# One core's hybrid decoder step: a list schedule that fixes the order on all five engines, and low parts of weights made by an accumulating DMA

## The chip, the cores and the metric

The kernel runs on one core of one Trainium2 chip. The metric is device microseconds of one execution. The kernel before takes 1466.67 us (median of 3 runs, 1466.05 to 1466.89). TensorE is called PE here, VectorE DVE, ScalarE ACT, GpSimd Pool and SyncE SP; every engine works through its own queue in order, and waits on semaphores for the others.

## The reference

A step of a decoder of two layers, on a prompt of 1024 tokens and on 8 sampled sequences of 4 new tokens each: 1056 tokens in all. The model is 1024 wide, the inside of a layer 2048.

```python
def lru_layer(x, conv_buf, h0, g, w_in, ...):          # layer 0 (Hawk)
    hn = rmsnorm(x, g)
    u = hn @ w_in                                      # 1024 -> 4096
    xb, z = u[..., :D_INNER], u[..., D_INNER:]
    xb, new_buf = causal_dwconv(xb, conv_buf, conv_w, conv_b)   # 4 taps
    y, h_last = rg_lru(xb, h0, w_a, b_a, w_i, b_i, lam)         # gates per block of 128, then a scan
    return x + (y * silu(z)) @ w_out, new_buf, h_last

def ccm_layer(x, conv_buf, g, w_in, b_in, ...):        # layer 1 (Conformer)
    u = rmsnorm(x, g) @ w_in + b_in                    # 1024 -> 6144
    v, gl, z = u[..., :D_INNER], u[..., D_INNER:2 * D_INNER], u[..., 2 * D_INNER:]
    c, new_buf = causal_dwconv(v * sigmoid(gl), conv_buf, dw_w, dw_b)   # 31 taps
    c = silu(layernorm(c, ln_g, ln_b))
    return x + (c * silu(z)) @ w_out + b_out, new_buf
```

A last RMSNorm follows. Everything is fp32.

## The kernel before, in words

**Tiling.** Channels lie on partitions, tokens on the free axis, in three chunks of 352. A weight matrix is cut into slabs of 128x1024 fp32 (512 KB): 48 for layer 0 (16 for the x branch, 16 for the gate z, 16 for the output) and 64 for layer 1 (16 each for v, its gate g and z, 16 for the output). Slabs are numbered in the order of their use, 0 to 47, 48 to 95, 96 to 111; `seq` holds them.

**Precision.** fp32 products are made of three matmuls in the fp32r type: weights and activations are each split into a high part h (the value rounded to fp32r by a copy) and a low part l (value minus high part), and `mm` (L241 on) adds h·h, h·l and l·h in PSUM. Nearly every matmul is 128x128 by 352 columns.

**Weights.** `w_load` (L211) starts a slab's load on SP into `wraw`. `w_conv` (L221) makes the high part `wh` with an ACT copy and the low part `wl` with a subtraction, on Pool but for three slabs of the start, which are on DVE. 38 slabs of layer 1 are "early": while layer 0 runs, `pre_load` (L328) loads each into `pre`, `pre_low` (L332) makes `preh` on ACT, subtracts it (19 on Pool, 19 on DVE, L336) and stores the low part to DRAM, `wld`; when such a slab is used, `w_load` fetches its low part too, and ACT copies it into `wl`.

**Layer 0.** 16 blocks of 128 channels. A block has an x branch (`xp`: 24 matmuls for each chunk, evacuated by `xb_evac`, L507, then the 4-tap convolution on DVE and ACT, L518 to L535, then `split`, L539, into `xcsh` and `xcsl`), a z branch (`zp`, evacuated with a Silu by ACT, L569), two gates (`gp`, per chunk, each of one 128x128 weight), sigmoids (L582), and a chain of DVE, ACT and Pool operations to the scan (`chain`, L586 to L620), whose result times silu(z) is split into `gsh` and `gsl`. Two blocks at a time go into the output (`op`, named by pair, group and chunk: `op2_4_0` is pair 2, output rows 4, chunk 0), which `out_evac` (L644) adds on DVE to the residual x.

**Layer 1.** Per block: g, v and z products (`yp` for the output), the 31-tap convolution (`tap`, L851; ACT, DVE and Pool share the products and sums), LayerNorm over all 2048 channels, then silu, gate and output in four groups, last the final norm (`y_unit`, L1122, `y_evac`, L1133).

**What sets the order.** The program is written as events, `at(t, fn)`, with times given by hand tables. `flush` (L168) calls them in the order of t. The start (t below 46) and the end are under `manual_schedule`, where engines keep the order of the calls; between them the framework's own scheduler orders each engine's instructions by its estimates.

Of the kernel before, what the change touches and what calls it, by code (L numbers as in the profile page):

```python
# [1333 lines left out]
```

## Time and profile before

| | |
|---|---|
| median of 3 runs | 1466.67 us (1466.05 to 1466.89) |
| span of the profiled execution | 1462.3 us |
| PE busy | 1398.0 us, 96% of the span, 8525 instructions |
| DVE busy | 1161.8 us, 79% |
| ACT, Pool busy | 872.4 and 872.5 us, 60% each |
| DMA over the span | 174.69 MB, mean 119 GB/s |

The profile is of one execution on the chip, 4.4 us less in its span than the median of the runs. "Busy" leaves out register, semaphore and DMA-issuing instructions. A row of windows gives, for a stretch of the span, its length and then busy time and instruction count of PE, of its weight loads (PEld), of DVE, ACT and Pool, then the clock granted to PE (1.00 is full), the busy share of the 16 DMA engines, and GB/s. A row of waits names the instruction that waited, by tile and line, what it waited for, and the total, count and longest in us. A row of one tile or line gives count, then shortest, middle and longest duration in ns and when it ran. A row of DMA issues ends in the middle time from issue to landing in us.

Layer 0 lies between about 34 and 640 us, layer 1's products, convolution and LayerNorm between 640 and 1260, and its output and the end behind that.

### The profile page before, as it was taken

To read this page: it belongs to the slowest core of one execution; us is meant where nothing else is said; L and a number is where in the kernel's file an instruction comes from. 1 tells how busy PE (TensorE), PEld (TensorE's weight loads), DVE (VectorE), ACT (ScalarE), POOL (GpSimd) and SP (SyncE) were. 2 spreads that over 40 slices of the span, in tenths; PEclk is the share of its full clock that TensorE was granted. 3 is DMA by queue.
4 is the path that set the end of the run, shared out by engine and by line. 5 is a ranking of instruction groups with operands and counts; after the bars stand their busy time and mean duration, and the time that the engine had idled before them with its cause. 6 is when DMAs were issued, how large, how long until landed. Compare 5 with 4: busy or idle time off the path is not lost.

```text
span 1462.3 us, 21525 instructions
## 1 busy us (share of the span) xinstructions
PE 1398.0 (96%) x8525; PEld 1367.2 (93%) x8525; DVE 1161.8 (79%) x1274; ACT 872.4 (60%) x1132; POOL 872.5 (60%) x479
## 2 busy tenths in 40 slices
PE   6998999999999999989999999999999999998997
PEld 6998989989899999989999989999999999998997
DVE  5777875675666767668989999999999997988525
ACT  5578466556565566757567676667677655533212
POOL 3544364345454545246689899998888996434233
PEclk9999999999999999999999999999999999999999
DMA  7011143343443342205623325333334224745203
GB/s 262 26 40 52 62 148 134 134 162 119 141 147 129 124 156 110 87 24 182 157 72 92 106 77 205 103 133 110 112 117 141 92 88 131 243 172 189 76 0 119
DMA packets 91829, 174.69 MB, mean 119 GB/s; under 512 B 41648, under 2 KB 53936, under 8 KB 91696
## 3 DMA queue, kind: packets, MB, share of 16 engines
q1 hardware_dynamic: 71152, 170.66, 34.0%
q10 hardware_dynamic: 20576, 2.66, 1.1%
q8 instruction: 67, 1.10, 0.3%
q14 instruction: 34, 0.28, 0.1%
HBM read 128.77 MB, written 46.22 MB: 120 GB/s over the span
## 4 chain that ended last, share of the span: by engine, by line
DVE 25%; PE 22%; POOL 5%; issue 3%; ACT 3%; DMA 2%; SPq 0%; POOLq 0%; DVEq 0%; ACTq 0%
DVE cv__9086 L870 2%; DVE cv__10890 L870 2%; DVE cv__9391 L870 2%; DVE cv__8787 L870 2%; POOL part__7852 L832 1%; DMA co<-od 1%; DVE cv__10602 L870 1%; POOL part__8145 L832 1%; DVE co L1089 1%; DVE cv__7518 L870 1%; DVE cpad L816 1%; DVE cv__9687 L870 1%; DVE cv__11218 L870 1%; DVE cv__8491 L870 1%; DVE co L1085 1%
## 5 line engine op out<-in xcount | busy, mean ns | idle before, releaser
L827 ACT ACTIVATE prod<-cpad,lay 128x1024 f32<-128x1024 f32 x119 | 135.7, 1147 | 64.1 <-POOL part__8145 L832 7.7
L530 DVE SCALAR_TENSOR_TENSOR acc<-pad,par,acc 128x1080 f32<-128x1080 f32 x32 | 62.5, 1961 | 39.6 <-ACT acc L523 39.2
L612 POOL COPY st_h<-r 128x1 f32<-128x1 f32 x16 | 17.4, 1090 | 103.6 <-DVE r L611 103.6
L336 POOL TENSOR_TENSOR pre<-pre,preh 128x1024 f32<-128x1024 f32 x19 | 49.5, 2607 | 48.2 <-ACT preh L335 37.4
L542 POOL TENSOR_TENSOR gsl<-zs,gsh 128x1056 fp32r<-128x1056 f32 x15 | 37.1, 2474 | 26.3 <-ACT gsh L541 23.3
L1152 POOL TENSOR_TENSOR sq<-sq 128x512 f32<-128x512 f32 (+2 forms) x20 | 19.0, 953 | 56.4 <-ACT sq L1148 56.2
L1148 ACT ACTIVATE sq<-x 128x512 f32<-128x512 f32 (+2 forms) x23 | 11.4, 501 | 67.5 <-DVE x L1138 63.6
L336 DVE TENSOR_TENSOR pre<-pre,preh 128x1024 f32<-128x1024 f32 x19 | 30.3, 1593 | 26.2 <-ACT preh L335 26.2
L541 ACT ACTIVATE gsh<-zs 128x1056 fp32r<-128x1056 f32 x15 | 16.3, 1084 | 56.2 <-DVE zs L618 56.2
L541 ACT ACTIVATE xcsh<-xc 128x1056 fp32r<-128x1056 f32 x16 | 17.4, 1086 | 53.6 <-DVE xc L535 53.6
L894 POOL TENSOR_TENSOR sum<-sum,co 128x1056 f32<-128x1056 f32 x13 | 35.0, 2689 | 23.9 <-DVE co L870 15.4
L1093 ACT ACTIVATE co<-co,par 128x352 f32<-128x352 f32 (+1 forms) x24 | 22.7, 970 | 41.8 <-DVE co L1089 41.8
L335 ACT ACTIVATE preh<-pre 128x1024 fp32r<-128x1024 f32 x38 | 40.0, 1052 | 12.8 <-DMA pre<-win 12.6
L400 POOL TENSOR_TENSOR hl<-hn,hh 128x352 fp32r<-128x352 f32 x24 | 25.4, 1062 | 36.5 <-ACT hh L397 31.0
L879 POOL TENSOR_TENSOR smp<-spad,lay 128x992 f32<-128x992 f32 x16 | 40.1, 2504 | 4.3 <-DVE spad L815 4.3
L944 POOL TENSOR_TENSOR ssq<-ssq,sq 128x1056 f32<-128x1056 f32 x14 | 40.6, 2897 | 0.0
L594 DVE TENSOR_TENSOR i<-i,xc 128x1056 f32<-128x1056 f32 x16 | 31.4, 1965 | 10.2 <-ACT i L582 9.1
L604 DVE TENSOR_TENSOR q<-q,i 128x1056 f32<-128x1056 f32 x16 | 21.7, 1356 | 21.9 <-ACT q L601 21.9
L611 DVE TENSOR_TENSOR_SCAN r<-a,q 128x1056 f32<-128x1056 f32 x16 | 37.7, 2357 | 0.6
L1105 POOL TENSOR_TENSOR nl<-co,nh 128x1056 fp32r<-128x1056 f32 x6 | 16.6, 2767 | 34.3 <-ACT nh L1101 31.8
L1085 DVE TENSOR_TENSOR co<-co,mub 128x1056 f32<-128x1056 f32 (+1 forms) x20 | 25.3, 1289 | 10.8 <-DMA co<-od 7.9
L393 DVE SCALAR_TENSOR_TENSOR hn<-x,par,pb 128x352 f32<-128x352 f32 x48 | 25.5, 573 | 9.6 <-PE pb L285 5.2
(5161 smaller groups left out, 6637.2 us busy)
## 6 DMA issues: line engine op xcount, KB each, us to landing
pre<-win SPq DMA_DIRECT2D x38, 512.0 KB, 3.7
wld<-pre SPq DMA_DIRECT2D x38, 512.0 KB, 2.8
zd<-z SPq DMA_DIRECT2D x16, 528.0 KB, 3.0
od<-co SPq DMA_DIRECT2D x12, 528.0 KB, 3.0
zr<-zd SPq DMA_DIRECT2D x12, 528.0 KB, 3.7
co<-od SPq DMA_DIRECT2D x12, 528.0 KB, 5.8
x<-xT SPq DMA_DIRECT2D x24, 176.0 KB, 4.6
x1d<-x SPq DMA_DIRECT2D x8, 528.0 KB, 6.1
```

What stands on the lines that cost most here:

```text
L335: act.activation(h, r, AF.Copy)
L336: (dve if early[i] % PRED == PRED - 1 else pool).tensor_sub(r, r, h.bitcast(F))
L530: dve.scalar_tensor_tensor(acc, pad[:, k:k + n], w, acc, op0=OP.mult, op1=OP.add)
L541: act.activation(h, src, AF.Copy)
L542: lo.tensor_sub(l, src, h.bitcast(F))
L611: dve.tensor_tensor_scan(h, B["a", s], B["q", s], 0.0, op0=OP.mult, op1=OP.add)
L827: act.activation(p, B["c", j][:, k:k + NP], AF.Identity, scale=dw(j, k), bias=P("dw_b", j) if k == 0 else 0.0)
L870: dve.scalar_tensor_tensor(o, x, dw(j, k), y, op0=OP.mult, op1=OP.add)
L879: pool.tensor_mul(t_.rearrange("p (b t w) -> p b t w", b=NB, t=NS), win, wb)
L894: pool.tensor_add(B["sum"], B["sum"], B["o", j])
L944: (dve if j in SQD else pool).tensor_add(B["ssq"], B["ssq"], q)
L1085: dve.tensor_sub(d, d, B["mu", 0][:, :C] if c == 0 else B["mub"][:, w])
```

## The change

**A list schedule.** All operations are now recorded first, each with its engine, the tiles that it reads and writes, and an estimated duration. `schedule` gives every operation a due time, backwards from its users, and then lets the engines take operations one at a time: at each step the operation that can start first, or one more urgent that can start within a short wait. What the planner has free (SBUF slots, PSUM banks) is part of it. The order that comes out is fixed for all five engines, in the whole program. Its costs are numbers in the file; it takes into account that some DVE and Pool operations share an access and cannot run at once (`lock`).

**Low parts by DMA.** Of the 74 slabs whose low part was a subtraction, 69 (from slab 5 on: 43 of layer 0, 6 of layer 1's first, 4 last z slabs, 16 of the output) now have it made by two steps: DVE writes minus the high part into `wl` (one multiplication by -1, one source), and Pool issues a DMA that adds `wraw` to it, SBUF to SBUF. For the 38 early slabs ACT writes minus the high part (scale -1 in the copy) into `preh`, and a Pool-issued DMA adds it to `pre`, which is stored to `wld` as before; at use `wld` is loaded straight into `wl`, without `wlow` and without the ACT copy.

**Beside it.** z is evacuated by three plain copies and one Silu over 1056 tokens (`z_silu`); each gate runs as one piece, 9 matmuls over the three chunks; 90 tiny "spare" activations load ACT tables ahead of their use; the pool `quick` is merged with the slots (44 in all). By instruction counts: DVE loses 19 subtractions and gains 69 multiplications, Pool loses 69 and 19 subtractions and gains 107 accumulating DMAs for weights and 10 for activations, ACT loses 38 copies and gains 16 Silus and the 90 spares, SP loads 38 low parts into another tile. The matmuls are the same ones.

The first place is PE at the gates of block 7, some 303 us into the run before. Names: `zp7_2` is z of block 7, chunk 2; `op2_4_0` is the output of pair 2 (blocks 4 and 5); `wh21`, `wl21` are the parts of slab 21; `gp7` is a gate of block 7 out of the split convolution `xcsh7`. Before:

```order
L246 MATMUL zp7_2__2859<-hh_153,wl20__2663 128x352
L244 MATMUL op2_4_0__2895<-gsh4_2035,wh21__2780 128x352
L245 MATMUL op2_4_0__2895<-gsl4_2036,wh21__2780 128x352
L244 MATMUL op2_4_1__2903<-gsh4_2035,wh21__2780 128x352
L245 MATMUL op2_4_1__2903<-gsl4_2036,wh21__2780 128x352
L244 MATMUL gp7_0__2997<-xcsh7_2848,gwh_2854 128x352
L246 MATMUL op2_4_0__2895<-gsh4_2035,wl21__2782 128x352
L244 MATMUL op2_4_0__2895<-gsh5_2405,wh21__2780 128x352
L245 MATMUL op2_4_0__2895<-gsl5_2406,wh21__2780 128x352
L246 MATMUL op2_4_0__2895<-gsh5_2405,wl21__2782 128x352
```

After, at the gates of the same block:

```order
L379 MATMUL op2_6_1_.0_3011<-gsh4.0_2115,wl21_.0_2794 128x352
L379 MATMUL op2_6_1_.0_3011<-gsh5.0_2530,wh21_.0_2721 128x352
L379 MATMUL op2_6_1_.0_3011<-gsl5.0_2557,wh21_.0_2721 128x352
L379 MATMUL op2_6_1_.0_3011<-gsh5.0_2530,wl21_.0_2794 128x352
L379 MATMUL gp7_0_0_.0_3019<-xcsh7.0_2940,gwh.7_2751 128x352
L379 MATMUL gp7_0_0_.0_3019<-xcsl7.0_2950,gwh.7_2751 128x352
L379 MATMUL gp7_0_0_.0_3019<-xcsh7.0_2940,gwl.7_2754 128x352
L379 MATMUL gp7_0_1_.0_3020<-xcsh7.0_2940,gwh.7_2751 128x352
L379 MATMUL gp7_0_1_.0_3020<-xcsl7.0_2950,gwh.7_2751 128x352
L379 MATMUL gp7_0_1_.0_3020<-xcsh7.0_2940,gwl.7_2754 128x352
L379 MATMUL gp7_0_2_.0_3021<-xcsh7.0_2940,gwh.7_2751 128x352
```

Before, the gate's first matmul stood 4 matmuls after block 7's z and cut into the output of pair 2, whose low-part matmuls followed it. Now it stands 48 matmuls after z, behind whole output products of pair 2, and a gate runs through all its chunks.

The second place is Pool in the same stretch of the program. `pre` rows are low parts of early slabs, `gsl6` the low part of block 6's gated output. Before:

```order
L542 TENSOR_TENSOR gsl6_2770<-zs6_2448,gsh6_2769 128x1056
L336 TENSOR_TENSOR pre_2731<-pre_2731,preh_2773 128x1024
L232 TENSOR_TENSOR wl21__2782<-wraw21__2665,wh21__2780 128x1024
L232 TENSOR_TENSOR wl22__2891<-wraw22__2784,wh22__2889 128x1024
L336 TENSOR_TENSOR pre_2918<-pre_2918,preh_2976 128x1024
L232 TENSOR_TENSOR wl23__3033<-wraw23__2893,wh23__3031 128x1024
```

After; a row with DMA is the issue of an accumulating transfer:

```order
L379 TENSOR_TENSOR gwl.7_2754<-graw.7_2633,gwh.7_2751 128x256
L379 DMA pre.10_2667<-preh.10_2789 128x1024
L379 DMA wl21_.0_2794<-wraw21_.0_2611 128x1024
L379 COPY st_h_75<-r6.0_2676 128x8
L379 COPY st_conv_74<-pad7.0_2635 128x3
L379 COPY st_conv_74<-pad7.0_2635 128x24
L379 COPY st_h_75<-r6.0_2676 128x1
L379 TENSOR_TENSOR gsl6.0_2902<-zs6.0_2526,gsh6.0_2865 128x1056
L379 DMA pre.11_2748<-preh.11_2867 128x1024
L379 DMA wl22_.0_2938<-wraw22_.0_2826 128x1024
```

Five subtractions of 128x1024 stood around `gsl6` before; now only DMA issues, gate weights, small copies of states and the same `gsl6` are left.

The third place is the end of layer 0 after the change, first on Pool, then on PE. `wl46` is the low part of the second output slab of the last pairs (6 and 7), `zp15_2` z of the last block, `op6_4_0` the first output product after it.

```order
L379 DMA wl44_.0_5781<-wraw44_.0_5543 128x1024
L379 DMA wl45_.0_5785<-wraw45_.0_5646 128x1024
L379 TENSOR_TENSOR gsl14.0_5932<-zs14.0_5813,gsh14.0_5928 128x1056
L379 DMA wl46_.0_5938<-wraw46_.0_5747 128x1024
L379 DMA wl47_.0_5971<-wraw47_.0_5750 128x1024
L379 DMA wl48_.0_5991<-wraw48_.0_5926 128x1024
```

```order
L379 MATMUL zp15_2_.0_5940<-hl.7_206,wh44_.0_5672 128x352
L379 MATMUL zp15_2_.0_5940<-hh.7_184,wl44_.0_5781 128x352
L379 MATMUL op6_4_0_.0_6016<-gsh12.0_5118,wh45_.0_5728 128x352
L379 MATMUL op6_4_0_.0_6016<-gsl12.0_5128,wh45_.0_5728 128x352
L379 MATMUL op6_4_0_.0_6016<-gsh12.0_5118,wl45_.0_5785 128x352
L379 MATMUL op6_4_0_.0_6016<-gsh13.0_5504,wh45_.0_5728 128x352
L379 MATMUL op6_4_0_.0_6016<-gsl13.0_5537,wh45_.0_5728 128x352
L379 MATMUL op6_4_0_.0_6016<-gsh13.0_5504,wl45_.0_5785 128x352
L379 MATMUL op6_4_0_.0_6016<-gsh14.0_5928,wh46_.0_5898 128x352
L379 MATMUL op6_4_0_.0_6016<-gsl14.0_5932,wh46_.0_5898 128x352
L379 MATMUL op6_4_0_.0_6016<-gsh14.0_5928,wl46_.0_5938 128x352
```

The number at the end of a tile's name counts tiles as the planner made them: `wl46` (5938) was made just ahead of `zp15_2` (5940), which begins 24 matmuls ahead of `op6_4_0`. The first use of `wl46` is the ninth matmul of `op6_4_0`, so 32 matmuls lie between them. Where the tiles of slabs 5, 9, 12, 47, 49 and 100 were made, between 35 and 50 matmuls lie ahead of the first use; for the others it is mostly more, between about 75 and 140.

The diff, cut to its core:

```diff
-NSLOT = 42  # tiles for whole rows of tokens
-NQUICK = 2
...
+WAHEAD = 1
+NSUB = 5
...
+T_TABLE, T_SEM, T_DMA0, T_DMAX, DMA_BW = 1.3, 0.055, 0.6, 1.25, 290.0e3
...
+    def schedule(self, caps):
...
+            o.due = o.at + SHIFT.get(o.key, 0.0)
+        for o in reversed(ops):
+            for s in o.succ:
+                o.due = min(o.due, s.due - o.dur - MARGIN - (T_DMA0 + T_DMAX + o.dma / DMA_BW if o.dma else 0))
+        queues = {e: sorted((o for o in ops if o.eng == e), key=lambda o: o.due) for e in ENG}
...
+        while todo:
+            best = None
+            lead = queues["PE"][0].due if queues["PE"] else 1e9
+            for e in ENG:
...
+                for i, o in enumerate(queues[e]):
+                    if i >= WIN[e] or (e != "PE" and o.due > lead + LOOK[e]):
+                        break
+                    if o.left:
+                        continue
+                    new = [t for t in o.acc if t.kind and t.place is None]
...
+                    s = max((max(free[e], last_end[e]) + x) if x else free[e], o.ready, c)
+                    if o.lock:
+                        s = max(s, lock)
+                    opts.append((s, x, o))
...
+                pick = opts[0]
+                for q in opts[1:]:
+                    back = T_TABLE if q[1] and pick[2].func and pick[2].func == table else 0.0
+                    if q[0] + q[2].dur + back + q[1] * 0.5 <= pick[0] + FIT[e]:
+                        pick = q
+                        break
+                s, x, o = pick
+                if best is None or s < best[0]:
+                    best = (s, x, o)
...
+            if o.dma:
+                d0 = max(dma, s + o.dur + T_DMA0 - 0.06)
+                dma = d0 + o.dma / DMA_BW
+                o.end = dma + T_DMAX
+            else:
+                o.end = s + o.dur + (0.17 if e == "PE" else 0.09)
+            last_end[e] = max(last_end[e], o.end)
+            if o.lock:
+                lock = s + o.dur - 0.05
...
+ENG = ("PE", "DVE", "Activation", "Pool", "SP")
+WIN = {"PE": 3, "DVE": 30, "Activation": 30, "Pool": 20, "SP": 12}
...
+MARGIN = 0.15
...
-        def flush(t_ordered=1e9):
-            todo = sorted(ev, key=lambda e: e[:2])
-            for engines, a, b in ((SU_E, -1e9, SU_M), ((), SU_M, t_ordered), (MAN, t_ordered, 1e9)):
-                with ExitStack() as order_:
-                    if engines:
-                        order_.enter_context(tc.manual_schedule(
-                            engines={getattr(mybir.EngineType, e) for e in engines}))
-                    for t_, _, fn, args in todo:
-                        if a <= t_ < b:
-                            fn(*args)
-            ev.clear()
...
+        def flush():
+            for i, (t_, _, fn, args) in enumerate(sorted(ev, key=lambda e: e[:2])):
+                plan.at, plan.event = t_, i
+                plan.key = fn.__name__ + (str(args[1]) if fn in (chain, conv0) else "")
+                fn(*args)
+            plan.schedule({"s": NSLOT, "g": NSMALL, "mm": 4, "aux": 4, "c": 1})
+            with tc.manual_schedule(engines={getattr(mybir.EngineType, e) for e in ENG}):
+                plan.emit(make, warm)
...
-                if i in early:
-                    lows[i] = slot(name=f"wlow{i}_", n=1024)
-                    sp.dma_start(lows[i], wld[early[i]])
...
                 if i in early:
-                    act.activation(l, lows.pop(i), AF.Copy)
+                    sp.dma_start(l.bitcast(F), wld[early[i]])
+                elif i < NSUB:
+                    (dve if split else pool).tensor_sub(l, r, h.bitcast(F))
                 else:
-                    (dve if split else pool).tensor_sub(l, r, h.bitcast(F))
+
+                    dve.tensor_scalar(l, h.bitcast(F), -1.0, None, op0=OP.mult)
+                    pool.dma_start(l.bitcast(F), r, accum_op=OP.add)
                 hls[i] = (h, l)
...
-            w_load(n + ahead + 1)
+            w_load(n + ahead + WAHEAD)
...
             r = B.pop(("pre", i))
             h = slot(FR, "preh", 1024)
-            act.activation(h, r, AF.Copy)
-            (dve if early[i] % PRED == PRED - 1 else pool).tensor_sub(r, r, h.bitcast(F))
+            act.activation(h, r, AF.Copy, scale=-1.0)
+            pool.dma_start(r, h.bitcast(F), accum_op=OP.add)
...
-            act.activation(B["zs", s][:, cs(c)], ps[:, :C], AF.Silu)
+            act.activation(B["zs", s][:, cs(c)], ps[:, :C], AF.Copy)
 
         def z_silu(s):
-            act.activation(B["zs", s][:, :C], B["zs", s][:, :C], AF.Silu)
-
-        def gate_unit(s, u):
-            g, c = divmod(u, NCH)
+            act.activation(B["zs", s], B["zs", s], AF.Silu)
+
...
+        def gate_units(s, g):
             h, l = B["gw", s]
             xh, xl = B["xcs", s]
-            ps = aux(f"gp{s}_{u}_")[:, :C]
-            mm(ps, [(h[:, g * 128:g * 128 + 128], l[:, g * 128:g * 128 + 128], xh[:, cs(c)], xl[:, cs(c)])])
-            if c == 0:
-                B["ri"[g], s] = slot(name=f"{'ri'[g]}{s}", n=NT)
-            act.activation(B["ri"[g], s][:, cs(c)], ps, AF.Sigmoid, bias=P("b_a" if g == 0 else "b_i", s))
-            if u == 2 * NCH - 1:
+            B["ri"[g], s] = slot(name=f"{'ri'[g]}{s}", n=NT)
+            ps = [aux(f"gp{s}_{g}_{c}_")[:, :C] for c in range(NCH)]
...
                 act.activation(B["q", s], B["q", s], AF.Sqrt)
+                if s not in late_z:
+                    z_silu(s)
```

More of the change, by code (lines that the diff above doesn't have):

```diff
@@ L1 @@
+import bisect
 import numpy as np
@@ new lines, with __init__, v @@
+class T:
+    def __init__(self, kind, name, shape, dt=F, real=None, phase=0, dram=False):
+        self.kind, self.name, self.dt, self.real, self.phase, self.dram = kind, name, dt, real, phase, dram
+        self.shape, self.left, self.free, self.place = shape, 0, 0.0, None
+        fake = [1 if q == 128 and i == (1 if dram else 0) else q for i, q in enumerate(shape)]
+        self.idx = np.arange(int(np.prod(fake))).reshape(fake)
+        self.users, self.hist = [], []
+    @property
+    def v(self):
+        return V(self, (), self.idx)
@@ new lines, with __init__ @@
+class Op:
+    __slots__ = ("eng", "parts", "due", "t", "pre", "succ", "left", "dur", "lock", "acc", "new", "dma", "start",
+                 "end", "func", "warm", "key", "kind", "n", "at", "ready", "tail")
+    def __init__(self, eng, at):
+        self.eng, self.at, self.parts, self.acc, self.pre, self.succ = eng, at, [], [], set(), []
+        self.dur, self.lock, self.dma, self.new, self.func, self.ready, self.warm = 0.0, False, 0, [], None, 0.0, False
+TABLE = {AF.Sigmoid: 1, AF.Exp: 2, AF.Tanh: 2, AF.Sqrt: 3, AF.Silu: 4}
@@ new lines, with __init__, __getattr__ @@
+class Eng:
+    def __init__(self, plan, name, real):
+        self.plan, self.name, self.real = plan, name, real
+    def __getattr__(self, op):
+        fn = getattr(self.real, op)
+        return lambda *a, **kw: self.plan.record(self.name, op, fn, a, kw)
+ENG = ("PE", "DVE", "Activation", "Pool", "SP")
+WIN = {"PE": 3, "DVE": 30, "Activation": 30, "Pool": 20, "SP": 12}
+LOOK = {"DVE": 20.0, "Activation": 20.0, "Pool": 20.0, "SP": 20.0}
+MARGIN = 0.15
+SHIFT = {}
+FIT = {"PE": 0.1, "DVE": 0.2, "Activation": 0.2, "Pool": 0.4, "SP": 0.1}
@@ L115, in build @@
     nc = tc.nc
-    pe, act, dve, pool, sp = nc.tensor, nc.scalar, nc.vector, nc.gpsimd, nc.sync
+    plan = Plan(tc)
+    pe, act, dve, pool, sp = (Eng(plan, n, e) for n, e in zip(
+        ("PE", "Activation", "DVE", "Pool", "SP"), (nc.tensor, nc.scalar, nc.vector, nc.gpsimd, nc.sync)))
     from contextlib import ExitStack
@@ new lines, in make @@
+        def make(t):
+            if t.kind == "c":
+                return pools["c"].tile(t.shape, t.dt, tag="lay", name=t.name)
+            if t.kind in ("s", "g"):
+                return pools[t.kind].tile([128, SLOT if t.kind == "s" else C], t.dt, tag=f"{t.kind}{t.place}_", name=t.name)
+            if t.kind == "mm":
+                return pools["mm"].tile(t.shape, F, tag=f"mm{t.place}_", name=t.name)
+            if px.get("open") != t.phase:
+                if "ctx" in px:
+                    px.pop("ctx").close()
+                px["ctx"], px["open"] = ExitStack(), t.phase
+                px["pool"] = px["ctx"].enter_context(tc.tile_pool(
+                    name=f"aux{t.phase}_", bufs=1, space=bass.MemoryType.PSUM, reuse_waits="tile"))
+            return px["pool"].tile(t.shape, F, tag=f"a{t.phase}_{t.place}_", name=t.name)
@@ new lines, in build @@
+        par = const("par", [128, PAR], F)
+        ident = const("ident", [128, 128], F)
+        ones = const("ones", [128, 1], F)
+        avg_r = const("avg_r", [128, 128], FR)
+        c8 = const("c8", [128, 2, KI], F)
+        st_conv = const("st_conv", [128, KI, (NB + 1) * (W0 - 1)], F)
+        st_h = const("st_h", [128, KI, NB + 1], F)
+        sm = const("sm", [128, 64], F)
+        x1d = scratch("x1d", [KD, 128, NT])
+        zd = scratch("zd", [KI, 128, NT])
+        od = scratch("od", [KI, 128, NT])
@@ L195, in build @@
+        spare = const("spare", [128, 2])
+        nss = const("nss", [128, NB * NS], F)
+        wld = scratch("wld", [NPRE, 128, D])
         lay = {}
@@ L694, in ev_gate @@
             nonlocal t
-            for u in range(2 * NCH):
-                at(t, gate_unit, s, u)
-                t += 0.45
+            for g in range(2):
+                at(t, gate_units, s, g)
+                t += 1.35
             ds_ = (0.5, 1.6, 4.8, 6.6, 7.2, 8.4, 9.8) if s < KI - 1 else (0.5, 1.6, 4.8, 6.6, 7.2, 10.9, 11.0)
+            if s not in z_end:
+                late_z.add(s)
             f = EARLY if s < 4 else STEADY if s < KI - 1 else 1.0
@@ L732, in build @@
         at(t, softplus)
-        for s in range(2):
-            at(SU_Z + 0.1 * s, z_silu, s)
         wi = 4
```

272 lines of the change are left out of this document (230 added, 42 removed).

## The prediction

> **What bounds the kernel now.** I read the page first: its first line and the busy times.
>
> ```profile
> span 1462.3 us, 21525 instructions
> PE 1398.0 (96%) x8525; PEld 1367.2 (93%) x8525; DVE 1161.8 (79%) x1274; ACT 872.4 (60%) x1132; POOL 872.5 (60%) x479
> ```
>
> PE is busy 96% of the span and the change leaves its matmuls alone, so all that can be won is what PE loses. Where it loses, the windows say (columns: stretch, length, busy time and count of PE, its weight loads, DVE, ACT, Pool; granted clock, DMA share, GB/s).
>
> ```profile
> 0.00:34.20 34.20, 23.26 (x115) 22.36 (x115) 19.02 (x28) 18.40 (x34) 12.01 (x18) 0.90 0.79 280
> 64.00:640.00 576.00, 548.83 (x3345) 540.90 (x3344) 398.26 (x437) 372.02 (x477) 267.28 (x190) 0.99 0.32 113
> 640.00:700.00 60.00, 57.80 (x355) 56.62 (x355) 47.76 (x89) 38.06 (x73) 33.41 (x27) 0.97 0.40 123
> 700.00:800.00 100.00, 100.00 (x625) 99.42 (x624) 93.26 (x80) 62.84 (x74) 79.21 (x33) 1.00 0.40 106
> 700.00:1220.00 520.00, 515.08 (x3158) 504.33 (x3157) 510.51 (x433) 345.02 (x399) 455.45 (x181) 1.00 0.36 113
> 1260.00:1370.00 110.00, 105.05 (x644) 102.64 (x644) 94.88 (x104) 41.73 (x43) 47.35 (x19) 1.00 0.54 193
> ```
>
> In 700 to 800 PE never stops: 100 us for 625 matmuls, 0.160 us each. I price every stretch by that. Layer 0 (64 to 640) needs 3345 x 0.160 = 535.2 of its 576 us: it loses 40.8, of which 576 - 548.83 = 27.2 are idle and 548.83 - 535.2 = 13.6 are matmuls that ran slowly. Layer 1 (700 to 1220) needs 505 of 520, with DVE busy for 510.5: DVE is its bound. 1260 to 1370 needs 103.0 of 110: 7 lost. So the place to argue about is layer 0. PE's waits there name the releasers (total, times, longest):
>
> ```profile
> PE xp__184 L244 <- ACT hh L412: 6.2, 1, 6.2
> PE op__1459 L244 <- DVE x L646: 3.5, 1, 3.5
> PE op__5881 L244 <- ACT gsh L623: 3.4, 1, 3.4
> PE gp__2997 L244 <- ACT xcsh L541: 3.4, 1, 3.4
> ...
> PE op__3671 L244 <- DVE x L646: 2.0, 1, 2.0
> ...
> PE op__5603 L244 <- DVE x L646: 1.9, 1, 1.9
> PE gp__1296 L244 <- ACT r L582: 1.8, 1, 1.8
> ...
> PE op__1861 L244 <- DVE x L646: 1.7, 1, 1.7
> PE op__2551 L244 <- ACT zs L569: 1.5, 1, 1.5
> ...
> PE op__3289 L244 <- ACT zs L569: 1.5, 1, 1.5
> ```
>
> Output products wait until DVE has evacuated a bank, a gate until DVE's convolution has been split. DVE is busy only 69% of layer 0; why is it late? The timeline around the gate of block 7 (start, length):
>
> ```profile
> 292.36 5.90 DVE L530 SCALAR_TENSOR_TENSOR acc<-pad,par,acc 128x1080 f32<-128x1080 f32 x2 [2.39 <-ACT acc L523]
> 293.67 3.44 POOL L336 TENSOR_TENSOR pre<-pre,preh 128x1024 f32<-128x1024 f32 x1
> 297.07 3.42 POOL L232 TENSOR_TENSOR wl__2782<-wraw__2665,wh__2780 128x1024 fp32r<-128x1024 f32 x1
> 298.36 3.22 DVE L533 SCALAR_TENSOR_TENSOR xc<-pad,par,acc 128x1024 f32<-128x1024 f32 x1
> 302.96 0.66 PE L244 MATMUL gp__2997<-xcsh,gwh 128*128 128x352 f32 x1 [3.44 <-ACT xcsh L541]
> ```
>
> and the same lines over the whole run (shortest, middle, longest ns), then the ten microseconds after:
>
> ```profile
> L530 DVE SCALAR_TENSOR_TENSOR acc<-pad,par,acc x32: 1327/1345/3531, 66.6 to 583.7; 128x1080 f32<-128x1080 f32 x32
> L533 DVE SCALAR_TENSOR_TENSOR xc<-pad,par,acc x16: 1271/1285/3339, 72.7 to 585.8; 128x1024 f32<-128x1024 f32 x16
> L336 POOL TENSOR_TENSOR pre<-pre,preh x19: 2388/2411/3485, 185.6 to 579.6; 128x1024 f32<-128x1024 f32 x19
> L336 DVE TENSOR_TENSOR pre<-pre,preh x19: 1206/1226/3423, 186.3 to 596.1; 128x1024 f32<-128x1024 f32 x19
> 300.00:310.00 10.00, 7.04 (x28) 7.04 (x29) 5.51 (x7) 5.99 (x7) 2.92 (x3) 0.66 0.56 210
> ```
>
> Three convolution steps of 1.3 us took 9.1 us because two Pool subtractions ran among them, and those took 3.4 instead of 2.4. The convolution is 5 us late, PE waits 3.4, and then its granted clock is 0.66 for ten microseconds: one wait costs twice.
>
> **The change part by part.** *Subtractions leave Pool (43 + 19 in layer 0) and DVE (19).* At 2.4 to 3.4 us the 62 are 149 to 211 of Pool's 267 us. Waits of the DVE kind (op 1459, gp 2997, op 3671, op 5603, op 1861) sum to 12.5 us. I take four fifths, 10.0: Pool keeps `gsl` and gate work to collide with, but the order after also puts a gate 48 matmuls behind z where it was 4. The ACT kind (gp 1296, op 2551, op 3289) is 4.8 us: the copy of z frees its bank without the Silu table, gates have whole output products ahead; three quarters, 3.6. `gsh` of the last block (3.4) is a chain's end that the change doesn't shorten: 0. The rest of the 27.2, 6.5 in small waits: half, 3.3. That is 16.9 of 27.2, 62%; of the 13.6 of slow matmuls, which follow waits, the same share is 8.4. Layer 0: -25.3 us. Its bounds are 0 and -40.8.
>
> *Negations come to DVE.* The groups of instructions give what goes (busy us, mean ns; then idle time ahead):
>
> ```profile
> L335 ACT ACTIVATE preh<-pre 128x1024 fp32r<-128x1024 f32 x38 | 40.0, 1052 | 12.8 <-DMA pre<-win 12.6 <-POOL wl__2663 L232 0.2
> L336 DVE TENSOR_TENSOR pre<-pre,preh 128x1024 f32<-128x1024 f32 x19 | 30.3, 1593 | 26.2 <-ACT preh L335 26.2
> ```
>
> No row shows a multiplication of one source with 1024 columns. The nearest is the subtraction at 1.2 us. In layer 0 43 x 1.2 = 52 replaces 19 x 1.6 = 30 and the collisions; DVE has 178 us free there, so 0 in itself. In 700 to 1220, where DVE is the bound, the order after has four (slabs 92 to 95): 4 x 1.2 = +4.8. In 1260 to 1370 12 x 1.2 = 14.4 makes DVE 109.3 of 110, less what collisions with Pool's subtractions cost it: I take -3 of the 7 lost, between -7 and +4.
>
> The Trainium skill (VectorE: DVE Perf Modes, The perf-mode tier table) says that a single-source fp32 operation between SBUF tiles runs at twice the rate. That would be an estimated 0.6 us a negation, +2.4 in place of +4.8, and the sum 2.4 us lower; no run here shows it yet.
>
> *Accumulating DMAs.* No row shows one. Plain transfers of the same 512 KB on SP's queue:
>
> ```profile
> L330 SPq DMA_DIRECT2D pre<-win x38: 327/328/611, 130.3 to 584.9; - x38
> pre<-win SPq DMA_DIRECT2D x38, 512.0 KB, 3.7
> wld<-pre SPq DMA_DIRECT2D x38, 512.0 KB, 2.8
> ```
>
> From the start of the negation to the landing: at least 1.2 + 0.33 (an issue as on SP) + 3.7 (a load) = 5.2 us; at most 1.2 + 2.4 (Pool as long as for the subtraction) + 3.7 + 2.8 (read, then written) = 10.1. I take 6.5, near the load. Of the slabs, seven are negated close to their use: 35 matmuls ahead for slabs 5 and 9, 32 for 46, 36 for 49, 38 for 100, 50 for 12 and 47, which is 5.6, 5.6, 5.1, 5.8, 6.1, 8.0 and 8.0 us. At 5.2 the waits add to 0.1, at 6.5 to 0.9 + 0.9 + 1.4 + 0.7 + 0.4 = 4.3, at 10.1 to 26.5. I take +4. The others have 12 us and more. What stands behind such a DMA on Pool, states and `gsl`, has no early reader. SP's stores to `wld` now wait for an accumulate instead of a subtraction, with weight loads queued behind; those are a slab ahead, and this rests on the landing time too.
>
> *ACT* loses 38 copies of a slab, 1.05 us each by the first row above (the same form), gains 90 tiny preloads; busy 60%, 0. *Start and the rest:* the first 34.2 us lose 15.8 (34.2 - 115 x 0.160), mostly the first loads, whose order changes; I see no net sign: 0, from -4 to +4. 640 to 700: 0.
>
> The sum is -25.3 + 4.8 - 3 + 4 = -19.5: span 1462.3 - 19.5 = 1442.8. The median lies 4.4 us above the span, so 1447. A measurement of this kernel can tell about 0.2%, 3 us.
>
> **The rivals.** *The DMA engines fill (slower).* In 64 to 640 they are busy 0.32 x 576 = 184 us for 113 GB/s x 576 us = 65.1 MB, so 0.524 MB costs 1.48 us of all 16. 392 us are free for 43 + 38 = 81 accumulates, 4.8 us each: the point from which it decides is 3.3 times a plain transfer. At 4 times, 5.9 us, they need 480: 184 + 480 - 576 = 88 us too much, and the kernel takes 1467 + 88 = 1555. For it: nothing here says what an accumulate costs, and it moves at least three streams where a store moves two. Against: three for two would be 1.5 times. Chance 0.16.
>
> *Low parts come late (gains given back).* A Pool instruction beside DVE's two-source ones took 3.4 instead of 2.4; if Pool's issue is held off by DVE as well, the landing is at the upper end, 10.1 us: the seven waits are 26.5, and the sum is -19.5 + 22.5 = +3, time 1470. Queues fixed in order on all engines make such lateness spread, since nothing overtakes. Against: the issue alone may touch nothing that DVE holds, and 12 us of lead cover most slabs. Chance 0.13. The Trainium skill (SBUF — State Buffer, Who interferes with whom) speaks for this rival: a DMA issued by GpSimd needs descriptors that it writes itself, and a DVE instruction that uses both port pairs, as a negation can, holds it off entirely until it ends. No trace here shows a DMA of this kind; the lengthened Pool subtraction agrees with the lock.
>
> *Nearly all of the loss goes.* If the order fits the chip, 0.9 x 40.8 = 37 in layer 0, 6 of the 7 late, 4 at the start, against +4.8: -42, time 1424. For it: all of the named waits have other work that could stand ahead. Against: a planner's durations must match collisions that here turn 1.3 us into 2.95. Chance 0.16.
>
> **How the numbers follow.** My forecast has 0.55, at 1447, by itself 1432 to 1462. The range leaves out the first rival (0.16) and little else: down to 1412 for the third, up to 1478 for the second. Faster by over 0.2%: 0.54 of the forecast, 0.16, and 0.04 of the second rival, 0.74. Within: 0.05, of the second. Slower: 0.16 + 0.04 + 0.01 = 0.21.
>
> **What would show it.** In the profile after: the convolution's steps at 1.3 us with longest ones below 2.5; no DVE releaser over 1 us in layer 0; PE's idle time there below 15 us with granted clock 1.00. The negation's row gives 1.2 or 0.6, the row of DMA issues the landing. If waits of PE name a DMA into `wl` for more than 10 us in all, the second rival has won; if the DMA share of layer 0 passes 0.8, the first. My forecast is wrong if layer 0's matmuls still lose over 30 us, or if DVE in layer 1 gains more than 10.

## The result, and the profile after

The changed kernel takes 1483.53 us (median of 4 runs, 1482.7 to 1488.14); the ratio to before is 1.0121, with a 95% interval of 1.0104 to 1.0138. It is slower by 1.2%, where I forecast 1447 and gave all slower outcomes together a chance of 0.21. Its profiled execution has a span of 1481.0 us, 18.7 more than before.

The page's first line and its busy times:

```profile
span 1481.0 us, 21862 instructions
PE 1399.9 (95%) x8525; PEld 1374.3 (93%) x8525; DVE 1105.8 (75%) x1324; ACT 848.7 (57%) x1188; POOL 728.9 (49%) x499
```

DVE has 56 us less to do, Pool 144 and ACT 24, and the kernel is longer. So I ask again what PE lost, and where. Windows of the kernel after (columns as in the prediction):

```profile
0.00:64.00 64.00, 49.42 (x284) 48.45 (x285) 48.93 (x101) 40.67 (x84) 29.89 (x42) 0.97 0.41 138
64.00:640.00 576.00, 539.47 (x3282) 532.71 (x3280) 349.35 (x423) 377.27 (x530) 161.70 (x195) 0.98 0.72 188
640.00:700.00 60.00, 50.42 (x280) 49.13 (x281) 44.30 (x90) 32.00 (x66) 24.09 (x26) 0.85 0.44 138
700.00:1220.00 520.00, 508.48 (x3105) 497.56 (x3104) 484.10 (x431) 308.36 (x381) 427.43 (x175) 0.99 0.40 114
1260.00:1370.00 110.00, 110.00 (x686) 109.74 (x686) 88.63 (x133) 48.37 (x65) 24.11 (x17) 0.98 0.81 249
```

Both kernels run the same matmuls, so the counts show who is ahead. The first 64 us are alike, 284 now and 286 in the kernel before:

```profile
0.00:64.00 64.00, 51.58 (x286) 49.57 (x287) 43.25 (x76) 36.35 (x76) 23.80 (x32) 0.95 0.43 154
```

In 64 to 640 the kernel after does 3282 where before did 3345, and in 640 to 700 280 where before did 355: 138 fewer at 0.160 us, 22 us behind at 700. From there to the end it wins 3 back: it loses 53 in 700 to 1220 and gains 42 in 1260 to 1370 alone. The whole loss is in layer 0 and at the change to layer 1. Not all of layer 0 is worse: against before, 150 to 250 us does 67 matmuls fewer and 550 to 650 does 84 fewer, but 250 to 550 does 45 more. The DMA share of layer 0 rose from 0.32 to 0.72.

PE's waits in the kernel after (the start's, in the first 64 us, left out):

```profile
PE op_.0_6016 L379 <- ACT gsh15.0_6006 L379: 9.2, 1, 9.2
PE st.5_6532 L379 <- DVE acc.7_6361 L379: 6.2, 1, 6.2
PE op_.0_1526 L379 <- DVE x_1.0_89 L379: 5.2, 1, 5.2
PE cv_.0_8663 L379 <- DVE cv_.0_8663 L379: 4.6, 1, 4.6
PE gp_.0_5584 L379 <- ACT xcsh14.0_5576 L379: 4.1, 1, 4.1
PE op_.0_1674 L379 <- DVE x_5.0_102 L379: 3.8, 1, 3.8
PE gp_.0_3053 L379 <- ACT r7.0_3039 L379: 3.4, 1, 3.4
...
PE op_.0_6016 L379 <- DMA wl_.0_5938<-wraw_.0_5747: 0.2, 1, 0.2
```

The waits of before are gone, and others of the same kinds have come: a bank that DVE evacuates late, a gate whose convolution is late. The last row is PE's only wait for an accumulating DMA: its readers nearly always had the low part in time. Nothing in this list accuses the transfers, and yet they stand behind some of it, as the timeline of 159 to 172 shows (rows of the engines concerned); how much of the loss is theirs is a question for the experiments.

```profile
159.23 0.69 DVE L379 TENSOR_SCALAR wl_.0_1588<-wh_.0_1565 128x1024 fp32r<-128x1024 f32 x1 [0.99 <-PE gp_.0_1570 L379]
...
160.22 0.87 POOL L379 DMA_DIRECT2D wl_.0_1588<-wraw_.0_1495  x1 [7.10 <-DVE wl_.0_1588 L379]
...
168.54 1.26 DVE L379 TENSOR_TENSOR q3.0_1652<-a3.0_1639 128x1056 f32<-128x1056 f32 x1 [3.40 <-DMA wl_.0_1588<-wraw_.0_1495]
...
171.01 0.52 DVE L379 TENSOR_TENSOR x_5.0_102<-op_.0_1632,x_5.0_102 128x352 f32<-128x352 f32 x1
...
171.58 0.66 PE L379 MATMUL op_.0_1674<-gsh0.0_1130,wh_.0_1439 128*128 128x352 f32 x1 [3.83 <-DVE x_5.0_102 L379]
```

`wl` 1588 is the low part of slab 11. DVE's `q3` has nothing to do with weights, but the planner gave it the place in SBUF where `wraw` 1495, the source of that transfer, lay. By the times that `schedule` computes, the transfer was to end, and the place to be free, 4.7 us after the issue; the transfer landed 8.3 us after it. DVE's order is fixed, so the evacuation of `x_5` stood behind `q3`, and PE waited 3.8 us for the bank. PE itself first read `wl` 1588 at 178 us, ten later than it landed. The same is met on ACT, whose outputs also take over such places; two of its waits, for the output of a gate (`r6`) and for minus a high part (`preh`):

```profile
ACT preh.12_2973 L379 <- DMA pre.11_2748<-preh.11_2867: 6.7, 1, 6.7
...
ACT r6.0_2676 L379 <- DMA wl_.0_2568<-wraw_.0_2379: 5.2, 1, 5.2
```

In 64 to 640 us ACT waited 59 us in 18 places for an accumulating transfer to land, and DVE 12 us in 6.

### The profile page after: what moved, and what is told of

Its sections match the earlier page's. It is cut to its first block, busy times and chain, and to the rows that moved or that the text cites. A ratio compares the mean times of both kernels' runs of the same rounds, so it can differ in the third digit from the quotient of the medians.

```text
span 1481.0 us, 21862 instructions
## 1 busy us (share of the span) xinstructions
PE 1399.9 (95%) x8525; PEld 1374.3 (93%) x8525; DVE 1105.8 (75%) x1324; ACT 848.7 (57%) x1188; POOL 728.9 (49%) x499
## 4 chain that ended last, share of the span: by engine, by line
PE 41%; DVE 13%; ACT 9%; DMA 6%; issue 3%; POOL 1%; SPq 0%; ACTq 0%; POOLq 0%; DVEq 0%
DVE cv_.0_7092 L379 2%; ACT L456 2%; DVE cv_.0_7484 L379 1%; DVE cv_.0_7747 L379 1%; DMA wl_.0_4865<-wraw_.0_4740 1%; DMA wl_.0_4115<-wraw_.0_3990 1%; DVE cv_.0_6779 L379 1%; DMA pre.27_4410<-preh.27_4459 1%; DMA wraw_.0_5290<-wout 1%; POOL part_.0_6987 L379 0%; PE vp_.0_6542 L379 0%; DMA wraw_.0_3790<-wout 0%; DVE cv_.0_8306 L379 0%; PE gp_.0_8699 L379 0%; DMA pre.33_5125<-preh.33_5196 0%
## 5 line engine op out<-in xcount | busy, mean ns | idle before, releaser
L379 DVE SCALAR_TENSOR_TENSOR cv_.0_6779<-cpad0.0_6537,lay.1_6000,cv_.0_6779 128x1024 f32<-128x1024 f32 x25 | 32.2, 1287 | 0.5
L379 DVE SCALAR_TENSOR_TENSOR cv_.0_7092<-cpad1.0_6660,lay.1_6000,cv_.0_7092 128x1024 f32<-128x1024 f32 x23 | 29.5, 1283 | 0.2
L379 DVE SCALAR_TENSOR_TENSOR cv_.0_10666<-cpad13.0_10173,lay.1_6000,cv_.0_10666 128x1024 f32<-128x1024 f32 x20 | 25.8, 1288 | 1.7 <-PE cv_.0_10666 L379 1.3
L379 DVE SCALAR_TENSOR_TENSOR cv_.0_8878<-cpad7.0_8476,lay.1_6000,cv_.0_8878 128x1024 f32<-128x1024 f32 x20 | 25.6, 1279 | 1.2 <-PE cv_.0_8878 L379 1.2
L379 DVE SCALAR_TENSOR_TENSOR cv_.0_9773<-cpad10.0_9289,lay.1_6000,cv_.0_9773 128x1024 f32<-128x1024 f32 x20 | 25.7, 1287 | 0.9 <-PE cv_.0_9773 L379 0.6
L379 DVE SCALAR_TENSOR_TENSOR cv_.0_10098<-cpad11.0_9595,lay.1_6000,cv_.0_10098 128x1024 f32<-128x1024 f32 x20 | 25.7, 1284 | 1.0 <-PE cv_.0_10098 L379 0.7
L379 DVE SCALAR_TENSOR_TENSOR cv_.0_9502<-cpad9.0_8940,lay.1_6000,cv_.0_9502 128x1024 f32<-128x1024 f32 x20 | 25.7, 1285 | 0.8 <-PE cv_.0_9502 L379 0.5
L379 DVE SCALAR_TENSOR_TENSOR cv_.0_10397<-cpad12.0_9951,lay.1_6000,cv_.0_10397 128x1024 f32<-128x1024 f32 x20 | 25.6, 1282 | 0.8 <-PE cv_.0_10397 L379 0.5
L379 DVE SCALAR_TENSOR_TENSOR cv_.0_10988<-cpad14.0_10518,lay.1_6000,cv_.0_10988 128x1024 f32<-128x1024 f32 x20 | 25.7, 1285 | 0.4
L379 DVE SCALAR_TENSOR_TENSOR cv_.0_8663<-cpad6.0_8052,lay.1_6000,cv_.0_8663 128x1024 f32<-128x1024 f32 x20 | 25.6, 1280 | 0.3 <-PE cv_.0_8663 L379 0.2
```

The costliest lines, as they stand in the source:

```text
L379: fn(*[real(a) for a in args], **{k: real(a) for k, a in kw.items()})
```

## The experiments

Two theories. **A (transfers):** the accumulating DMAs cost more than planned, hold their tiles, and fixed queues hand that on. **B (order):** the list order loses by itself, at the start of layer 0, at its end and in layer 1, however low parts are made. The ratios below are to the kernel before, on the same chip, with 95% intervals. Where two of the kernels are compared, the difference in us is that of their ratios times 1467, since the chips were not all the same.

**The list schedule alone, all low parts by subtraction** (e1).

```diff
-NSUB = 5
+NSUB = 112
-            act.activation(h, r, AF.Copy, scale=-1.0)
-            pool.dma_start(r, h.bitcast(F), accum_op=OP.add)
+            act.activation(h, r, AF.Copy)
+            (dve if early[i] % 2 == 1 else pool).tensor_sub(r, r, h.bitcast(F))
```

> The list schedule alone: every low part is again a subtraction (slabs on Pool, the 38 early ones half on Pool and half on DVE, planned by the same planner), low parts of early slabs still loaded straight into their tile. Theory A (transfers: accumulating DMAs land later than planned, hold their tiles and fill the DMA engines, and the fixed queues pass that on) expects 1440 to 1465 us, DMA share of layer 0 back near 0.4, and under 15 us between the planner's time and the chip's in layer 0. Theory B (order: the fixed order loses by itself at the start of layer 0, at its end and at the start of layer 1) expects 1475 or more, with the 9 us wait for the last block's gsh and the wait of the first layer-1 statistic still there.

Measured: 1473.35 us, 1.0028 (1.0009 to 1.0047). Between the two: faster than the changed kernel by 14 us, so the transfers have a part, but not faster than before, so the order brings nothing by itself. The wait for the last block's `gsh` was 11.8 us here, that of the first statistics of layer 1 4.5: B's places are real.

**The transfers alone, in the kernel before** (e2): its own scheduler and tables.

```diff
-                    (dve if split else pool).tensor_sub(l, r, h.bitcast(F))
+                    dve.tensor_scalar(l, h.bitcast(F), -1.0, None, op0=OP.mult)
+                    pool.dma_start(l.bitcast(F), r, accum_op=OP.add)
```

(from slab 5 on, and the early slabs as in the change)

> The kernel before with its own scheduler and hand tables, and only the low parts changed: slabs from 5 on by a multiplication by -1 on DVE and an accumulating DMA, early ones by ACT and an accumulating DMA. Theory A expects it slower than before, 1475 to 1500 us, with PE or the engines before it waiting for such transfers. Theory B expects 1440 to 1466: Pool and DVE no longer collide, and the order is not the planner's.

Measured: 1530.79 us, 1.0425 (1.0386 to 1.0465): A's side, and beyond its range. Here PE does wait for the transfers; the first rows of its waits:

```profile
PE op__4395 L249 <- DMA wl__4278<-wraw__4165: 6.8, 1, 6.8
...
PE op__3653 L249 <- DMA wl__3538<-wraw__3425: 5.5, 1, 5.5
PE op__4022 L249 <- DMA wl__3907<-wraw__3794: 5.3, 1, 5.3
PE op__2542 L249 <- DMA wl__2427<-wraw__2314: 5.3, 1, 5.3
```

There are 14 such waits with 41.6 us in all. In the kernel before, a slab's low part is begun one slab ahead, and that lead does not cover the transfer. So the list schedule is worth 45 us once the transfers are there: it makes the lead. It is worth nothing without them. (Its scheduler orders PE anew when low parts change, so this is not before's order to the row.)

**Only the early slabs by transfer, in the list schedule** (e4; `NSUB = 112` alone) and **only the others** (e3; the early subtraction of e1 alone).

> The changed kernel with one constant changed: low parts of slabs by subtraction on Pool, only the 38 early ones by accumulating DMA (38 of 107 such transfers left). Theory A expects a time between the list schedule with subtractions alone and the changed kernel, about a third of the way from the first: 1455 to 1475. Theory B expects 1478 to 1490, as the changed kernel.

> The changed kernel, with the early low parts by subtraction again (half Pool, half DVE) and the slabs by accumulating DMA: the fourth corner beside the list schedule with none, with early only and with both. If the two parts add up, the list with none (1473) plus the slabs' 22 us: 1492 to 1498. If the slabs' transfers hurt only in company with the early ones (shared engines, tiles), 1470 to 1480.

Measured: early only 1461.06 us, 0.9946 (0.9928 to 0.9963); slabs only 1457.35, 0.9922 (0.9898 to 0.9947). The second misses both its ranges on the fast side; the first lies inside theory A's range, but not between the two kernels, as A has it. Either part alone makes the list schedule faster, by 12 and 16 us, and both together make it slower, by 14. So neither is bad in itself. Taking subtractions from Pool and DVE does pay, as the prediction argued, and something that comes with both kinds of transfers together eats it.

**The early slabs alone, in the kernel before** (e8).

> The kernel before with its own order, and only the 38 early low parts by accumulating DMA. Theory A says that a transfer hurts where its reader or its tile is needed soon; the early slabs are read hundreds of us later, so only the stores and tiles behind them can suffer: 1460 to 1475 us, against 1531 with all of them. If accumulating transfers as such crowd the DMA engines, a third of the 62 us: 1485 or more.

Measured: 1490.00 us, 1.0137 (1.0110 to 1.0163). Theory A's range was too good, and the time lies in the range for transfers that crowd the engines. The profile shows that only in part. In 250 to 550 us PE waited 24 us, in 19 small pieces for ACT, DVE and Pool, none of them for a transfer. ACT's gate work did wait for one, five times and 14.2 us over the run, and at 312.7 us such a wait of 2.7 us stands just ahead of a wait of PE for that gate (2.1 us). For the other pieces no transfer is seen behind them, and the scheduler had also put PE in another order, so how much of this is the transfers' is not shown.

**The planner's price of a transfer corrected** (e5): the same instructions, another order.

```diff
-                dma = d0 + o.dma / DMA_BW
-                o.end = dma + T_DMAX
+                acc = e == "Pool"
+                dma = d0 + o.dma / DMA_BW * (1.55 if acc else 0.85)
+                o.end = dma + T_DMAX + (1.5 if acc else 0.3)
```

(and due times 2.5 us earlier for accumulating ones)

> The changed kernel with only the planner's price of transfers changed towards the trace: an accumulating DMA takes 2.8 us of the DMA engines (planned 1.8) and lands 1.5 us later, a plain one 1.54 us and 0.3 later; due times 2.5 us earlier for accumulating ones. Nothing but the order changes. Theory A expects a good part of the planner's 31 us slip in layer 0 to go: 1455 to 1475. Theory B expects no gain: 1478 to 1490.

Measured: 1461.08 us, 0.9947 (0.9927 to 0.9968): some 25 us faster than the changed kernel, as A expects. The windows of 250 to 550, of the changed kernel and then of this one:

```profile
250.00:550.00 300.00, 293.38 (x1814) 290.74 (x1813) 187.97 (x225) 197.81 (x275) 94.45 (x112) 0.99 0.87 231
```

```profile
250.00:550.00 300.00, 298.92 (x1869) 298.44 (x1868) 194.51 (x233) 205.12 (x286) 86.69 (x116) 1.00 0.90 237
```

The DMA engines are as busy as before, 0.90, and PE hardly stops: 1869 matmuls are 299 us of work. ACT now waits 23 us for accumulating transfers in 64 to 640 and DVE 2, where it was 59 and 12. A high DMA share is not what costs here; an order that does not expect it is.

**Plain copies in place of accumulations** (e9): the same order, tiles and issues as in the changed kernel; it leaves out the addition.

```diff
-                    pool.dma_start(l.bitcast(F), r, accum_op=OP.add)
+                    pool.dma_start(l.bitcast(F), r)
```

(and likewise in `pre_low`)

> The changed kernel with the same order, tiles and issues, but all 107 transfers are plain copies of the same bytes on the same queue instead of accumulations (this leaves out the addition: low parts of weights are the raw slab, or minus the high part). If what the accumulations cost is that each occupies the DMA engines for 2.8 us where a plain transfer of the size takes 1.5, and so crowds them, the DMA share of 250 to 550 us falls from 0.87 to about 0.6, transfers land in 4 to 5 us and the time falls to 1455 to 1468. If it is the chain of steps (multiplication, issue on Pool, landing) or the fixed order whatever the transfer takes, it stays at 1478 or more.

Measured: 1460.48 us, 0.9948 (0.9931 to 0.9966), with a DMA share of 0.67 in 250 to 550 us. This is the cleanest of them, since nothing but the kind of transfer differs: the two ratios differ by 0.0173, so 25 us of 1467 is what accumulating costs beyond copying, in this order. The waits for these transfers in 64 to 640 us fell to 17 us on ACT and 1.7 on DVE, while the wait for `gsh15` stayed (9.7 us). The queue on which Pool issues, in the changed kernel and in this one (packets, MB, share of 16 engines over the span):

```profile
q0 software_dynamic: 15408, 56.11, 20.2%
```

```profile
q0 software_dynamic: 15408, 56.11, 9.9%
```

These 107 are all the transfers that Pool issues in the run, 69 of slabs and 38 of early ones; the 10 for activations that I named with the change are not among its instructions. 0.202 x 1481.0 / 107 = 2.80 us of all 16 engines for one accumulation, 0.099 x 1458.5 / 107 = 1.35 for one copy. Over all rows of transfers into `wl`, the quickest landed 4.5 us after the issue against 2.8, the middle one 6.2 against 4.1. And the chain of 159 to 172 is there again, row for row, smaller:

```profile
158.71 0.57 POOL L379 DMA_DIRECT2D wl_.0_1588<-wraw_.0_1495  x1 [7.03 <-DVE wl_.0_1588 L379]
...
165.42 1.26 DVE L379 TENSOR_TENSOR q3.0_1652<-a3.0_1639 128x1056 f32<-128x1056 f32 x1 [1.74 <-DMA wl_.0_1588<-wraw_.0_1495]
...
168.46 0.66 PE L379 MATMUL op_.0_1674<-gsh0.0_1130,wh_.0_1439 128*128 128x352 f32 x1 [2.15 <-DVE x_5.0_102 L379]
```

The landing came 1.6 us sooner, DVE waited 1.7 us less, and so did PE. The issue on Pool is shorter too, 0.57 for 0.87; this run does not part that from the occupation of the engines.

**The end of layer 0 put in another order** (e6; with the corrected prices).

```diff
-FINAL = "X14 X15 G14 O12 Z14 G15 Z15".split()
+FINAL = "X14 X15 G14 Z14 G15 O12 Z15".split()
```

> The kernel with the corrected transfer prices, and one string changed: at the end of layer 0 the last z but one and both last gates come ahead of an output product (X14 X15 G14 Z14 G15 O12 Z15 for X14 X15 G14 O12 Z14 G15 Z15). Theory A alone (only transfers cost) expects no difference from the corrected prices: 1458 to 1464 us. Theory B (a part of the loss is the order itself, at the end of layer 0) expects the 8.5 us wait for the last block's gsh to fall below 3 us and the time to 1448 to 1456.

Measured: 1453.63 us, 0.9895 (0.9872 to 0.9918): 8 us better than with the prices alone, as B expects. The wait for `gsh15` is gone, but a part of it came back as this:

```profile
PE op_.0_6016 L380 <- DMA wl_.0_5982<-wraw_.0_5790: 7.2, 1, 7.2
```

`wl` 5982 is the low part of slab 46, one of the seven short leads of the prediction: with the chain of the last block out of its way, it is the last thing to arrive.

**Early slabs by transfer, with the corrected prices** (e7: e4 and e5 together).

> The corrected transfer prices, with slabs by subtraction on Pool and only the 38 early ones by accumulating DMA. If what slabs by DMA cost is the wrong price alone, the price should now make no difference between this and all by DMA: 1457 to 1465 us. If a slab by DMA costs in itself, beyond the price, this is faster than all by DMA with the right price: 1445 to 1456.

Measured: 1465.40 us, 0.9974 (0.9960 to 0.9989), not faster than with the wrong prices (0.9946), if anything 4 us slower, and no faster than all by transfer with the right ones (0.9947). So slabs by transfer cost nothing in themselves that this shows. A better price is not a better order everywhere.

**Half of the early slabs by transfer** (e14): every second early one by a subtraction on DVE.

> The changed kernel with every second early low part by a subtraction on DVE, the others and all slabs by accumulating DMA: 62 transfers in layer 0, where 0 gave 1473 us, 38 gave 1461, 43 gave 1457 and 81 gave 1484. If the loss is a crowd that begins only where the engines are nearly full, at an expected share of about 0.77 in 250 to 550 us the time stays near the better ends, 1452 to 1462. If each transfer beyond the first ones costs alike, half way from 1457 to 1484: 1466 to 1475.

Measured: 1472.39 us, 1.0022 (1.0004 to 1.0039). The number lies where a cost alike for each transfer would put it, but the profile is no even cost: in 350 to 550 us, at a DMA share of 0.78, PE was busy for 200.00 of 200 us. Against e3, which is 15 us faster, it falls 70 matmuls behind in 150 to 350 us and 37 in 550 to 640. At the first place the chain of slab 11 is met again (`q3` waits 2.7 us for the transfer, PE 3.1 for `x_5`); at the second one evacuation cost 7.6 us where it cost 3.3 in e3. Each set of costs gives another order, and orders differ by some 10 us at places like the second. So I take no difference under 10 us between two planned orders as the price of an operation; e9, where the order is the same, is not touched by that.

**The best parts together:** slabs by transfer, early ones by subtraction, the new end of layer 0 (e11), and the same with the corrected prices (e13).

> Slabs by accumulating DMA, early low parts by subtraction, the planner's prices as in the change, and the end of layer 0 with the last gates ahead of an output product. The two gains are at different places (transfers at 150 to 560 us, the last block's gates at 560 to 640), so they should add: 1457 less some 8 us, 1446 to 1452. If the wait only moves, as the wait for gsh became one for a transfer, 1454 or more.

> As the one before, with the corrected prices. With a third of the transfers gone the engines are not crowded (share 0.66), so the price should make little difference: within 4 us of the one before. If the wait at the last output product is for a low part that is made too late, the earlier due times for accumulations take it away: 3 to 7 us faster than the one before.

Measured: 1447.28 us, 0.9852 (0.9817 to 0.9887), and 1450.27 us, 0.9876 (0.9845 to 0.9906). The two gains add; the price makes no difference that can be told, and the 3 to 7 us that the second might have won did not come. The first is faster than the kernel before by 1.5%, and 39 us faster than the changed one.

**The plan against the chip.** `schedule` computes the end of its own plan: 1433.6 us for the changed kernel, the same for e9, 1441.7 for e1, 1419.4 for e11. Nine kernels with the list order (e1, e3 to e7, e9, e11 and e13) have spans 23 to 30 us longer than their plans; the changed kernel's is 47 longer and e14's 38. So 14 us of e11's gain over the changed kernel stand in the plan, as do 7 and 10 of the 12 and 16 us that e4 and e3 won over e1, and what the plan did not see is the 20 us or so by which the changed kernel falls out of the row.

## Why the prediction was wrong, point by point

**What bounds the kernel** held: all that moved was PE's lost time. DVE, Pool and ACT were all less busy and the kernel was slower, so their busy times do not tell it.

**Layer 0, -25.3: the step that failed.** It became +10 (63 matmuls fewer by 640), and "640 to 700: 0" became +12. Layer 0's stretch lost 40.8 us before and 50.9 after, 36.5 idle and 14.4 of slow matmuls, beyond the 30 that I had named as the sign of being wrong. I had taken shares of named waits, four fifths of one kind and three quarters of another, as if waits were a list from which a change strikes lines. By the listed waits of 64 to 640, PE waited 12.1 us for DVE and 14.8 for ACT before, and 14.1 and 13.7 after, without the wait for `gsh15`, which runs from 633.3 to 642.5 and so adds 6.7 in this stretch. The places changed, and the sum rose. What the step left out is that a new order has weak places of its own. They stood in the plan: by the starts that `schedule` computes, PE idles 28 us between 64 and 640, as much as the 27.2 before; 12.1 of them are ahead of op 6016 and 5.4 ahead of op 1526, where the chip waited 9.2 and 5.2, and another 4.4, which became 6.2, are ahead of `st` 5 in 640 to 700. The 9.2 us for `gsh15`, where I had left the 3.4 of before as it was, comes from the place of the last block's gates. Before, four of their six chunks stood ahead of z of block 14; now the first gate stands behind all 72 matmuls of it and the second 24 further on, behind a chunk of z of block 15, so the chain to `gsh15` begins some 12 us later. The order shows that without a run. e6 and e11 moved the gates forward and the wait went. The other part is the transfers, 25 us by e9: of the 43 us between the -21 that I had for 64 to 700 (the -25 and the +4 of the transfers) and the +22 that came, they make up over half.

**Collisions.** The removed subtractions did pay, 12 to 16 us in the list schedule (e1 against e4 and e3), not far above the 10 us by which orders differ. But the test that I named, the convolution's longest steps below 2.5 us, fails: Pool's `gsl` still meets it, as at 578 us in the kernel after:

```profile
578.06 4.02 DVE L379 SCALAR_TENSOR_TENSOR xc14.0_5571<-pad14.0_5303,par,acc14.0_5499 128x32 f32<-128x32 f32 x2
578.59 2.41 POOL L379 TENSOR_TENSOR gsl13.0_5537<-zs13.0_5157,gsh13.0_5504 128x1056 fp32r<-128x1056 f32 x1
...
583.25 0.66 PE L379 MATMUL gp_.0_5584<-xcsh14.0_5576,gwh.14_5328 128*128 128x352 f32 x1 [4.12 <-ACT xcsh14.0_5576 L379]
```

One step of 32 columns and one of 1024 took 4.0 us together where 1.45 is the usual, and the gate waited 4.1.

**Negations, +4.8 in layer 1.** The row says 0.69 us in the middle, not 1.2. That is near the 0.6 that I had estimated from the rate in the Trainium skill (VectorE: DVE Perf Modes, The perf-mode tier table). Layer 1 lost 8.5 us all the same (53 matmuls), and not to them: DVE was busy 484 of 520 us, no longer the bound, and PE waited 4.6 us for one convolution row (`cv` 8663) and 2.8 for z of block 14, in the order of the list, in e1 as well as in the change. 1260 to 1370 gained 6.7, where I had -3.

**Accumulating DMAs, +4: the landing nearly right, the victim wrong, and the cost too small by six times.** I had taken 6.5 us from the negation to the landing, within 5.2 to 10.1; at slab 11 it was 9.3 (159.23 to 168.5), and in the middle about 7: 0.7 for the negation and 6.2 from the issue. I asked only when the reader needs the low part, and found seven short leads; PE waited 0.2 us for them. I did not ask when the source's place is needed again. That is where the late landing struck, on ACT (59 us of waits) and DVE (12), with evacuations and gates behind, and with plain copies 25 us of the time went.

**The rivals.** *The DMA engines fill* had the right sum: with the measured 2.80 us it gives 184 + 81 x 2.80 = 411 of 576, a share of 0.71, and 0.72 was measured. But I let it decide only from 3.3 times a plain transfer, when the engines have no time left, and the price was 1.9 times (2.80 against 1.48). *Low parts come late*, at 1470, came nearest, with the right last step (in fixed queues lateness spreads) and the wrong first one: Pool's issue was hardly held off. Two issues and a negation of the kernel after:

```profile
179.95 0.86 POOL L379 DMA_DIRECT2D pre.0_1602<-preh.0_1744  x1 [1.19 <-ACT preh.0_1744 L379]
...
180.48 1.26 POOL L379 DMA_DIRECT2D wl_.0_1749<-wraw_.0_1590  x1
...
180.95 0.68 DVE L379 TENSOR_SCALAR wl_.0_1784<-wh_.0_1752 128x1024 fp32r<-128x1024 f32 x1
```

The second issue took 1.26 us instead of 0.86, but it began while the first still ran; from the end of that (180.81) it took 0.93. Of Pool's 66 DMA issues in 150 to 560 us four took over 1 us, and all four began behind one that still ran; from its end three of them took 0.9 and one 1.21. Six others had a negation beside them and took 0.86 to 0.88. The Trainium skill (SBUF — State Buffer, Who interferes with whom) states that such a negation can lock Pool out until it ends; these rows show some 0.3 us that could be it, once, so it cost little here. *Nearly all of the loss goes* did not happen, in any run: 1447 was the best, the forecast number, but by another order and without the early transfers.

**What stays open:** how the 25 us of e9 divide between the engines' longer occupation, the later landing and Pool's longer issue, and how much of e8's loss in the kernel before is the transfers'.

## What to carry to other kernels

When a change makes a result later, ask not only when the reader needs it but when the memory of its source and its target is wanted again: in queues with a fixed order the first to suffer can be an instruction that never touches the data. A planner's price for an operation that it has not yet used has to be measured: here 1.8 us of the DMA engines and 4.7 us from issue to landing of a slab (the middle) were planned, 2.8 and 6.2 were measured, and the order with the corrected price won some 25 us. And a sum over the old kernel's waits does not hold when the whole order is new: cost the new order's own weak places, such as the last chain of a stage. A planner that computes starts has them as a list, and the idle time in it can be read before any run.

## What the hardware showed that I had not expected

- An accumulating DMA of 512 KB from SBUF to SBUF occupied the 16 DMA engines for 2.80 us in the mean (the changed kernel) and landed in 4.5 us at best; a plain copy of the same bytes on the same queue took 1.35 and landed in 2.8 (e9).
- The issue of an accumulation took 0.86 us on Pool in the middle, that of the plain copy 0.53; one on SP's queue took 0.33.
- With the DMA engines 0.90 busy over 300 us, PE ran 1869 matmuls in them, a loss of 1 us (e5).
